# The first projections of a hybrid decoder step: token squares taken from the feature blocks of x, four like passes for v, and later row loads

## The chip, the cores and the metric

The kernel runs on one core of one Trainium2 chip. The metric is the time of one launch on the device, in microseconds (us), as the median of several runs. Beside the runs there is one profiled execution, whose trace is read here; it has its own time.

## The reference, cut to what matters

One decoder layer is computed for 256 prompt tokens and 64 sampled tokens (8 sequences of 8), 320 tokens together, with a model width of 2048. Everything is float32.

```python
def rms_norm(x, w):
    y = xf * lax.rsqrt(jnp.mean(xf * xf, axis=-1, keepdims=True) + EPS)
    return (y * w).astype(x.dtype)

def decoder_layer(x, ...):
    h = rms_norm(x, p["norm_mix_pre"])
    proj = h @ p["w_in"]                       # columns: u | v | z | x,B,C | dt
    gate_out, chunk_v = chunk_spatial_gate(a_u, a_v, ...)   # v = layer_norm(gelu(a_v))
    ssm_out, ... = ssd_mixer(z, xbc, dt_raw, ...)           # xbc: causal conv of width 4, silu
    mix = concat([gate_out, ssm_out]) @ p["w_out"]
    x = x + rms_norm(mix, p["norm_mix_post"])
    f, ... = conv_ffn(rms_norm(x, p["norm_ffn_pre"]), ...)
    x = x + rms_norm(f, p["norm_ffn_post"])
```

What the change touches is the beginning: the norm of x, the 2048 columns of `a_v` (2048 to 4095 of `w_in`), the layer norm of v, and the conv inputs B and C.

## The kernel before, in words

**Layout.** Activations are held transposed: features on the 128 partitions, the 320 tokens along the free axis. x comes in as `xT`, 16 blocks of 128 features by 320 tokens (160 KB each), and a second time by token as `x_tok` for the sum of squares. A product with float32 accuracy is made from three passes in a faster format: each operand is split into a high part (a rounded copy) and a low part (the difference), and `accumulate` (line 128) issues high by high (L130), high weights by low x (L131) and low weights by high x (L132), each 128x128 weights against 128x320. `slab` (line 112) loads up to 512 KB of weights by SyncE (SP, L117), makes the rounded copy on ScalarE (ACT, L119) and the difference on VectorE (DVE, L121). Raw, high and low weights have three buffers each, so a load waits until the difference of the third slab before it is made, and a rounded copy waits until TensorE (PE) has used the third one before it.

**A pass.** `project` (line 154) multiplies all 16 blocks of h with 512 (or 256) columns of a weight matrix: 192 matmuls for 512 columns, into four PSUM banks (tag `mm`, four buffers). After each column block the evacuation `evac` is written out; after each slab `tick` advances one background task in the list `bg`. The norm's factor of a token, `r1`, is not needed for the matmuls, since it is multiplied in when a bank is evacuated: `scaled` (line 336) multiplies by `r1` on DVE (L340) and applies the activation on ACT (L341).

**Order.** The program is written by one Python thread with background generators and priorities (`tc.high_priority`, `first`); a scheduler then fixes a list of instructions for each engine, and each engine works through its list in order. `tc.issue_after` makes an instruction wait for another.

**The beginning.** The first pass over v (columns 2048 to 2559) loads x block by block in `x_ready` (L538), splits it on ACT (L543) and DVE (L544), and between these loads the token rows of x (L559), six loads of 256 or 512 KB. `x_squares` squares them on ACT with a running sum (L564), and `rsqrt_of` makes `r1` in eleven small DVE operations; `spread` (L269) turns it with three PE transposes and `r1` is copied out of PSUM on ACT (L271). The first pass does not wait for it: its four banks stay full (`late`), and the next 256 columns go to four banks of the other PSUM pool (`spare=True`, `misc`). When `r1` is there, the task `with_r1` issues the parameter loads (`params`, L329 to L332) and the four late evacuations. Then come 256 more columns and two passes of 512, with `turned` (12 PE transposes by L576, three copies by L577) after each group of 512 columns.

**After that** come the conv inputs B and C (`conv_proj`: the evacuation writes a padded row `pad` with three buffers, L393 and L394, then ACT L398 and three DVE steps L400), beside them the layer norm of v in the background (`layer_norm`, bn_stats L617, L635, L636), with its rows loaded by GpSimd (POOL, L628), then dt, the first x heads, and the gate's passes. The gate's weights for the first group (`gate_mix`, L653 to L655) are loaded by POOL as well. Both the first rows and the first gate weights wait for one small POOL copy of `r1` (`behind_r1`, L334).

Of the kernel before, what the change touches and what calls it, by code (L numbers as in the profile page):

```python
# [9 lines left out]
F32 = mybir.dt.float32  # L10
# [7 lines left out]
P = 128  # L18
NP = 256
# [15 lines left out]
def hybrid_step(  # L35
# [118 lines left out]
    def project(w, c0, evac, width=512, spare=False, late=None, quiet=0, ready=None, small=0, after=None, ahead=1, rate=1, more=None, held=None):  # L154

        nb = width // P
        ps = [misc(f"ps_{c0}_{j}") if spare else mm.tile([P, 512], F32, tag="mm", name=f"ps_{c0}_{j}") for j in range(nb)]
# [20 lines left out]
        there = None  # L178
        for cut in cuts[:ahead] if ready else []:
            there = ready(*cut)  # L180
        for i, (k0, nk) in enumerate(cuts):
            with tc.issue_after(there or after) if there or after and i > 1 else nullcontext():
                if ready and i + ahead < len(cuts):
                    there = ready(*cuts[i + ahead])
# [140 lines left out]
    behind_r1 = []  # L325

    def params():
        with tc.issue_after(slab_load[-1]):
            sp.dma_start(prm, cols)  # L329
            sp.dma_start(sst, sconv)  # L330
            sp.dma_start(bias_bc, ssm_dt_bias[0:1, :].broadcast_to([P, NH]))
            sp.dma_start(a_bc, ssm_a_log[0:1, :].broadcast_to([P, NH]))  # L332
        there = tp.tile([P, 1], F32, tag="there", name="r1_there", bufs=1)
        behind_r1.append(pool.tensor_copy(there, r1[:, 0:1]).ins)  # L334
# [37 lines left out]
    with ExitStack() as mctx:  # L372
# [6 lines left out]
        def conv_proj(c0, k0, out, soon=0):  # L379
# [138 lines left out]
        with tc.tile_pool(name="gp", bufs=1) as gp:  # L518
# [14 lines left out]
            x_split = []  # L533

            def x_ready(k0, nk):
                with tc.high_priority(offset=100000):
                    cs = slice(KD + NT * k0 if k0 else 0, KD + NT * (k0 + nk))
                    sp.dma_start(flat[:, cs], xT[:, cs])  # L538
                    for _ in range({4: 1, 6: 1, 8: 1, 10: 1, 12: 2}.get(k0, 0)):
                        load_by_token()  # L540
                    for kt in range(k0, k0 + nk):
                        x = xf[:, kt, :]
                        x_split.append(act.activation(hT[0][:, kt, :], x, AF.Copy, scale=pre[:, kt:kt + 1]).ins)  # L543
                        dve.scalar_tensor_tensor(out=hT[1][:, kt, :], in0=x, scalar=pre[:, kt:kt + 1],  # L544
                                                 in1=hT[0][:, kt, :].bitcast(F32), op0=ALU.mult, op1=ALU.subtract)


            ssq = gp.tile([P, 3, 2], F32, name="ssq1")
            pool.memset(ssq, 1.0)
            xp = acc.rearrange("p k n -> p (k n)")[:, :2 * D].rearrange("p (c d) -> p c d", c=2)  # L550
            by_tok = [(xp[:, c, D // 2 * i:D // 2 * (i + 1)], slice(0, P), slice(P * c, P * c + P), c, i)
                      for c in range(2) for i in range(2)]
            by_tok += [(t.rearrange("p k n -> p (k n)")[64:, :D // 2], slice(64, P), slice(NP, NT), 2, i) for i, t in enumerate((bT, cT))]
            to_load = list(by_tok)

            def load_by_token():
                if to_load:
                    t, _, rows, _, i = to_load.pop(0)
                    sp.dma_start(t, x_tok[rows, D // 2 * i:D // 2 * (i + 1)])  # L559

            def x_squares():
                for n, (t, at, _, c, i) in enumerate(by_tok):
                    with tc.high_priority(offset=50000), tc.issue_after(x_split[min(15, 11 + n)]):
                        act.activation(t, t, AF.Square, accum_out=ssq[at, c, i:i + 1])  # L564
                with first():
                    ss1 = gp.tile([P, 3], F32, name="ss1")
                    dve.tensor_reduce(out=ss1, in_=ssq, axis=mybir.AxisListType.X, op=ALU.add)
                    return rsqrt_of(ss1, 1.0 / D, 3)
# [12 lines left out]

            late = []
            project(w_in, V0, lambda j, ps: scaled(ps, AF.Gelu, vfs[0][:, j, :]), ready=x_ready, small=4, ahead=0, late=late)
            with tc.high_priority(offset=100000):
                while to_load:
                    load_by_token()

            def with_r1():
                yield
                yield  # L590
# [7 lines left out]
            task = with_r1()  # L598
            next(task)
            bg.append(task)  # L600
# [47 lines left out]
            def gate_mix(g, uf, res):  # L648
# [3 lines left out]
                with tc.issue_after(behind_r1[0]):  # L652
# [652 lines left out]
```

## Time and profile before

| | |
|---|---|
| runs (median; lowest, highest) | 1795.4 us; 1794.08, 1796.96 (3 runs) |
| profiled execution, its own time | 1796.46 us |
| span of its instructions | 1794.8 us |
| granted TensorE clock, mean | 0.998 |
| PE, DVE, ACT, POOL busy | 99%, 66%, 44%, 15% |
| moved by DMA | 306.45 MB, 171 GB/s on average |

The profile gives, for each engine, the busy time and the number of instructions; PEld is the weight load of TensorE, which runs beside its matmuls. A view of windows gives the same for chosen stretches, in brackets the number of instructions that touch the stretch. A line of the timeline reads: start, duration, engine and line, operation, output and inputs, shapes, count, and in square brackets the idle time before it with what ended it. A matmul's own record is about 0.31 us long, but matmuls overlap, so PE's rate is read from the number of records in a stretch and not from its busy share.

### The profile page before, as it was taken

How to read it: one execution, taken by the hardware profiler on the slowest of the kernel's cores; microseconds unless marked ns; L12 is line 12 of the kernel's file. 1: busy time of each engine (PE TensorE's matmuls, PEld its weight loads, DVE VectorE, ACT ScalarE, POOL GpSimd, SP SyncE). 2: the span in 40 equal slices, each digit the busy share in tenths (PEclk: the TensorE clock that was granted, in tenths of full speed). 3: DMA queues.
4: the chain of work that ended last, by engine and by line, in shares of the span. 5: the costliest groups of instructions: out<-in, count | busy, mean ns of one | idle time of the engine just before them, and what ended most of it. 6: DMA issues, size and time to landing. Idle time of an engine off the chain costs nothing.

```text
span 1794.8 us, 31242 instructions
## 1 busy us (share of the span) xinstructions
PE 1777.0 (99%) x12235; PEld 1744.6 (97%) x12235; DVE 1186.1 (66%) x2051; ACT 796.4 (44%) x1105; POOL 268.0 (15%) x591
## 2 busy tenths in 40 slices
PE   8999999999999999999999999999999999999998
PEld 8999999999989898999999999999999999999997
DVE  5449565556867778677876575767666575656565
ACT  6444454334535354445645443443434343433334
POOL 1102110000220111003222212121101020101004
PEclk9999999999999999999999999999999999999999
DMA  8645544445764654454565656566554444444442
GB/s 274 185 142 178 174 139 154 153 152 163 242 195 157 192 159 153 138 170 150 161 198 199 206 177 192 191 193 213 173 190 152 150 155 153 151 148 153 154 152 98
DMA packets 230210, 306.45 MB, mean 171 GB/s; under 512 B 17488, under 2 KB 153008, under 8 KB 229872
## 3 DMA queue, kind: packets, MB, share of 16 engines
q1 hardware_dynamic: 218416, 284.51, 49.8%
q10 hardware_dynamic: 10160, 15.47, 2.3%
q0 software_dynamic: 1488, 4.49, 0.9%
q8 instruction: 96, 1.57, 0.4%
q14 instruction: 50, 0.41, 0.1%
HBM read 286.85 MB, written 17.58 MB: 170 GB/s over the span
## 4 chain that ended last, share of the span: by engine, by line
PE 89%; issue 6%; DMA 3%; DVE 1%; ACT 1%; SPq 0%; POOL 0%; DVEq 0%; POOLq 0%; ACTq 0%
PE ps L130 18%; PE ps L132 18%; PE ps L131 18%; PE pd L130 10%; PE pd L132 10%; PE pd L131 10%; PE y_ps L862 1%; DMA wraw<-in_w_in 1%; DMA vt<-in_xT 1%; PE yo_ps L815 1%; PE sg L669 0%; PE up_ps L1155 0%; PE tsum L261 0%; PE xt_ps L361 0%; DVE wlo L121 0%
## 5 line engine op out<-in xcount | busy, mean ns | idle before, releaser
L121 DVE TENSOR_TENSOR wlo<-wraw,whi 128x1024 fp32r<-128x1024 f32 x472 | 587.6, 1245 | 393.9 <-ACT whi L119 391.3
L119 ACT CAST whi<-wraw 128x1024 fp32r<-128x1024 f32 x472 | 494.1, 1047 | 719.7 <-PE ps L131 429.0
L130 PE MATMUL ps<-h_hi,whi 128*128 128x320 f32 x2528 | 785.2, 311 | 5.2 <-ACT whi L119 3.6
L131 PE MATMUL ps<-h_lo,whi 128*128 128x320 f32 x2528 | 780.5, 309 | 0.0
L132 PE MATMUL ps<-h_hi,wlo 128*128 128x320 f32 x2528 | 779.2, 309 | 0.4 <-DVE wlo L121 0.4
L130 PEld LDWEIGHTS ps<-h_hi,whi 128*128 128x128 f32 x2528 | 474.8, 188 | 11.7 <-issue 5.3
L131 PEld LDWEIGHTS ps<-h_lo,whi 128*128 128x128 f32 x2528 | 475.1, 188 | 1.5 <-issue 0.5
L132 PEld LDWEIGHTS ps<-h_hi,wlo 128*128 128x128 f32 x2528 | 474.5, 188 | 1.8 <-DVE wlo L121 1.3
L130 PE MATMUL pd<-fhi,whi 128*128 128x320 f32 x704 | 217.4, 309 | 0.0
L132 PE MATMUL pd<-fhi,wlo 128*128 128x320 f32 x704 | 217.3, 309 | 0.0
L131 PE MATMUL pd<-flo,whi 128*128 128x320 f32 x704 | 217.3, 309 | 0.0
L130 PE MATMUL pd<-ohi,whi 128*128 128x320 f32 x448 | 140.5, 314 | 0.0
L131 PE MATMUL pd<-olo,whi 128*128 128x320 f32 x448 | 138.9, 310 | 0.0
L132 PE MATMUL pd<-ohi,wlo 128*128 128x320 f32 x448 | 138.6, 309 | 0.0
L131 PEld LDWEIGHTS pd<-flo,whi 128*128 128x128 f32 x704 | 132.2, 188 | 0.7
L132 PEld LDWEIGHTS pd<-fhi,wlo 128*128 128x128 f32 x704 | 132.2, 188 | 0.0
L130 PEld LDWEIGHTS pd<-fhi,whi 128*128 128x128 f32 x704 | 132.2, 188 | 0.0
L213 DVE TENSOR_TENSOR acc_ffn<-acc_ffn,pd 128x320 f32<-128x320 f32 x160 | 77.1, 483 | 34.6 <-PE pd L132 33.6
L130 PEld LDWEIGHTS pd<-ohi,whi 128*128 128x128 f32 x448 | 84.1, 188 | 4.0 <-issue 2.5
L132 PEld LDWEIGHTS pd<-ohi,wlo 128*128 128x128 f32 x448 | 84.1, 188 | 0.6 <-issue 0.6
L131 PEld LDWEIGHTS pd<-olo,whi 128*128 128x128 f32 x448 | 84.2, 188 | 0.2 <-issue 0.2
L1052 POOL COPY ptf<-pad 128x2 f32<-128x2 f32 x88 | 21.0, 240 | 408.1 <-DVE pad L1040 407.6
(292 smaller groups left out, 1572.1 us busy)
## 6 DMA issues: line engine op xcount, KB each, us to landing
wraw<-in_ffn_w_up SPq DMA_DIRECT2D x176, 512.0 KB, 3.5
wraw<-in_w_in SPq DMA_DIRECT2D x144, 512.0 KB, 3.5
wraw<-in_ffn_w_down SPq DMA_DIRECT2D x88, 512.0 KB, 3.3
wraw<-in_w_out SPq DMA_DIRECT2D x64, 512.0 KB, 3.3
st<-in_state_ssm SPq DMA_DIRECT2D x64, 256.0 KB, 3.6
out_ssm_state_sample<-st ACTq DMA_DIRECT2D x32, 256.0 KB, 2.4
cs<-dacs_d SPq DMA_DIRECT2D x16, 320.0 KB, 3.6
xr<-in_xT SPq DMA_DIRECT2D x4, 640.0 KB, 4.6
```

What stands on the lines that cost most here:

```text
L119: act.copy(hi[:, :m], raw[:, :m])
L121: dve.tensor_tensor(out=lo[:, :m], in0=raw[:, :m], in1=hi[:, :m].bitcast(F32), op=ALU.subtract)
L130: pe.matmul(ps, whi, xhi, start=first, stop=False)
L131: pe.matmul(ps, whi, xlo, start=False, stop=False)
L132: return pe.matmul(ps, wlo, xhi, start=False, stop=last).ins
L213: dve.tensor_tensor(out=acc[:, nb, :], in0=acc[:, nb, :], in1=ps[:, :NT], op=ALU.add)
L815: pe.matmul(ps_yo[row:row + 32, :256], cms[:, 4 * h + i, :], st[h][:, 256 * r:256 * r + 256], start=i == 0, stop=i == 3, tile_position=(0, ...
L862: pe.matmul(ps[64 * i:64 * i + 64, cols], w(hl), x(hl, m, cpx), tile_position=(0, 64 * i), **flags)
L1052: pool.tensor_copy(ptf[:, k, :], pad[:, 256:258])
```

## The change

- x is loaded once, as `xT`, in more and earlier pieces; `x_tok` is no longer read by the kernel. The squares are made from the feature blocks: ACT squares two blocks at a time into `acc` (8 operations of 128x640), DVE adds them up (7 of 128x640 and one of 128x320), and `token_sums` adds over the partitions with three PE matmuls of one column each.
- The four groups of v are four like passes of 512 columns in the `mm` banks. The first one evacuates after `r1`, which is made within it: the new argument `before=tick` advances the task with `spread` and `params` ahead of its first evacuation.
- The transposes of group g come after the pass of group g+1, the last ones inside the pass of B, as a background task ahead of the layer norm.
- The layer norm's rows wait for the third group of v, the gate's first weights for the first block of B, each through a small POOL copy (`behind`).
- Odd blocks of B and C take up to three more padded buffers, cut from a buffer of `xs`.

```diff
@@ project
-                if kt == KD - 1 and late is None:
+                if kt == KD - 1 and late is None and not before:
+            if before and kt == KD - 1:
+                if js[0] == 0:
+                    before()
+                for j in js:
+                    evac(j, ps[j])
...
+        to_make = list(cuts) if ready else []
         for i, (k0, nk) in enumerate(cuts):
+            with tc.issue_after(after) if after and i > 1 else nullcontext():
+                while to_make and len(cuts) - len(to_make) <= max(i + ahead, (i + 1) * (i == len(cuts) - 2)):
+                    ready(*to_make.pop(0))
@@ conv
-                pad = op.tile([P, LP], F32, tag="pad", name="pad", bufs=3)
+                pad = spare_pads.pop(0) if spare_pads and j % 2 else op.tile([P, LP], F32, tag="pad", name="pad", bufs=3)
@@ x_ready
-                    sp.dma_start(flat[:, cs], xT[:, cs])
-                    for _ in range({4: 1, 6: 1, 8: 1, 10: 1, 12: 2}.get(k0, 0)):
-                        load_by_token()
+                    for at in {0: (0,), 1: (1,), 2: (2,), 3: (3,), 4: (4, 6), 6: (8, 10), 8: (12, 14)}.get(k0, ()):
+                        x_load(at, 1 if at < 4 else 2)
...
+                with tc.high_priority(offset=50000):
+                    for kt in range(k0 - k0 % 2, k0 + nk - 1, 2):
+                        act.activation(acc[:, kt:kt + 2, :], xf[:, kt:kt + 2, :], AF.Square)
+                        if kt:
+                            dve.tensor_tensor(out=acc[:, 0:2, :], in0=acc[:, 0:2, :], in1=acc[:, kt:kt + 2, :], op=ALU.add)
@@ with_r1
-                    r = x_squares()
+                    dve.tensor_tensor(out=acc[:, 0, :], in0=acc[:, 0, :], in1=acc[:, 1, :], op=ALU.add)
+                    r = rsqrt_of(token_sums(acc[:, 0, :]), 1.0 / D, 3)
                 yield
                 spread(r, r1)
                 params()
-                for ev, j, ps in late:
-                    ev(j, ps)
@@ the passes of v
-            project(w_in, V0 + 512, lambda j, ps: scaled(ps, AF.Gelu, vfs[1][:, j, :]), width=256, spare=True)
-            turned(0, vfs[0])
-            project(w_in, V0 + 768, lambda j, ps: scaled(ps, AF.Gelu, vfs[1][:, 2 + j, :]), width=256)
-            turned(1, vfs[1])
+            v_pass(0, vfs[0], ready=x_ready, small=4, ahead=0, before=tick)
+            v_pass(1, vfs[1])
+            turned(0, vfs[0])
             for g in range(2, 4):
                 vf = gp.tile([P, 4, NT], F32, tag="vf", name="vf", bufs=2)
-                project(w_in, V0 + 512 * g, lambda j, ps: scaled(ps, AF.Gelu, vf[:, j, :]))
-                turned(g, vf)
+                v_pass(g, vf)
+                turned(g - 1, vfs[-1])
+                vfs.append(vf)
+                if g == 2:
+                    behind(vf[:, 3, 0:1])
+            def last_turned():
+                yield
+                turned(3, vfs[-1])
+            bg.append(last_turned())
@@ layer_norm, gate_mix, the conv passes
-                        with tc.issue_after(behind_r1[0]):
+                        with tc.issue_after(after_v[0]):
...
-                with tc.issue_after(behind_r1[0]):
+                with tc.issue_after(after_v[-1]):
...
+            spare_pads = op.tile([P, 4, NT], F32, tag="xs", name="xs_pads", bufs=2).rearrange("p k n -> p (k n)")
+            spare_pads = [spare_pads[:, LP * i:LP * i + LP] for i in range(3)]
             conv_proj(B0, 16, lambda j: bT[:, j, :], 50000)
+            behind(bT[:, 0, 0:1])
```

More of the change, by code (lines that the diff above doesn't have):

```diff
@@ L152, in finish, with project @@
             tick()
-    def project(w, c0, evac, width=512, spare=False, late=None, quiet=0, ready=None, small=0, after=None, ahead=1, rate=1, more=None, held=None):
+    def project(w, c0, evac, width=512, late=None, before=None, quiet=0, ready=None, small=0, after=None, ahead=1, rate=1, more=None, held=None):
         nb = width // P
-        ps = [misc(f"ps_{c0}_{j}") if spare else mm.tile([P, 512], F32, tag="mm", name=f"ps_{c0}_{j}") for j in range(nb)]
+        ps = [mm.tile([P, 512], F32, tag="mm", name=f"ps_{c0}_{j}") for j in range(nb)]
         if more:
@@ L323, in hybrid_step @@
     sst = cp.tile([P, 24, NB, 3], F32, name="sst")
-    behind_r1 = []
     def params():
@@ L332, in params @@
             sp.dma_start(a_bc, ssm_a_log[0:1, :].broadcast_to([P, NH]))
-        there = tp.tile([P, 1], F32, tag="there", name="r1_there", bufs=1)
-        behind_r1.append(pool.tensor_copy(there, r1[:, 0:1]).ins)
     def scaled(ps, func, out):
@@ L549, in hybrid_step @@
[L549 to L568, printed above, removed]
+                with tc.high_priority(offset=50000):
[3 more added lines that the diff above has]
+                            dve.tensor_tensor(out=acc[:, 0:2, :], in0=acc[:, 0:2, :], in1=acc[:, kt:kt + 2, :], op=ALU.add)
@@ L580, in hybrid_step @@
             first_raw += [vf.rearrange("p k n -> p (k n)")[:, 512 * i:512 * i + 512] for vf in vfs for i in range(2)]
[L582 to L586, printed above, removed]
             def with_r1():
-                yield
-                yield
+                yield from repeat(None, 7)
                 with first():
-                    r = x_squares()
+                    dve.tensor_tensor(out=acc[:, 0, :], in0=acc[:, 0, :], in1=acc[:, 1, :], op=ALU.add)
+                    r = rsqrt_of(token_sums(acc[:, 0, :]), 1.0 / D, 3)
                 yield
@@ L595, in with_r1, with behind, v_pass @@
                 params()
[L596 to L601 removed]
+                yield
+            after_v = []
+            def behind(x):
+                there = tp.tile([P, 1], F32, tag="there", name="v_there", bufs=1)
+                after_v.append(pool.tensor_copy(there, x).ins)
+            r1_task = with_r1()
+            bg.append(r1_task)
+            def v_pass(g, vf, **more):
+                project(w_in, V0 + 512 * g, lambda j, ps: scaled(ps, AF.Gelu, vf[:, j, :]), **more)
+            v_pass(0, vfs[0], ready=x_ready, small=4, ahead=0, before=tick)
+            v_pass(1, vfs[1])
             turned(0, vfs[0])
[L603 to L604 removed]
             for g in range(2, 4):
                 vf = gp.tile([P, 4, NT], F32, tag="vf", name="vf", bufs=2)
[L607 to L608 removed]
+                v_pass(g, vf)
[4 more added lines that the diff above has]
+            def last_turned():
+                yield
+                turned(3, vfs[-1])
+            bg.append(last_turned())
             def layer_norm():
```

16 lines of the change are left out of this document (6 added, 10 removed).

## The prediction

> **What bounds the kernel now.** I read the page first, then PE's waits, then windows cut at the ends of the passes, then the timeline at each wait.
>
> ```profile
> span 1794.8 us, 31242 instructions
> PE 1777.0 (99%) x12235; PEld 1744.6 (97%) x12235; DVE 1186.1 (66%) x2051; ACT 796.4 (44%) x1105; POOL 268.0 (15%) x591
> PE 89%; issue 6%; DMA 3%; DVE 1%; ACT 1%; SPq 0%; POOL 0%; DVEq 0%; POOLq 0%; ACTq 0%
> ```
>
> PE is busy all the time and is 89% of the chain that ended last. The change takes no work from PE; it adds three small matmuls. So all it can win is time in which PE stood still, and the list of PE's waits says how much there is in the part that it touches:
>
> ```profile
> PE ps L130 <- ACT whi L119: 3.6, 3, 2.5
> PE vt_ps L576 <- ACT vf L341: 1.6, 1, 1.6
> PE ps L130 <- DVE pad L394: 1.3, 1, 1.3
> ```
>
> The windows give the same as a balance. They are cut at the ends of the four v groups, of B and of C (the columns: window, its length, each engine's busy time with its instructions, granted clock, DMA share, GB/s).
>
> ```profile
> 4.90:40.35 35.45, 31.53 (x192) 29.47 (x193) 21.89 (x40) 23.77 (x39) 3.32 (x7) 0.95 0.87 288
> 40.35:70.60 30.25, 30.17 (x209) 29.72 (x208) 12.69 (x18) 13.92 (x20) 5.66 (x11) 1.00 0.80 231
> 70.60:102.00 31.40, 29.77 (x206) 29.38 (x205) 14.30 (x16) 11.97 (x16) 0.00 (x0) 1.00 0.44 135
> 102.00:131.70 29.70, 29.70 (x206) 29.45 (x205) 12.87 (x14) 11.62 (x15) 0.00 (x0) 1.00 0.47 142
> 131.70:161.40 29.70, 29.70 (x206) 29.45 (x205) 26.89 (x52) 11.28 (x14) 3.09 (x8) 1.00 0.56 165
> 161.40:191.10 29.70, 28.41 (x194) 28.17 (x193) 24.45 (x44) 14.50 (x22) 9.48 (x20) 1.00 0.65 208
> 191.10:219.20 28.10, 28.10 (x194) 28.10 (x193) 15.65 (x21) 11.85 (x18) 5.41 (x13) 1.00 0.49 151
> ```
>
> The last window is a pass without any wait: 192 matmuls (two more touch its edges) in 28.10 us, 0.146 us each. The window 102.00:131.70 is such a pass with its 12 transposes: 29.70. Against these, the first pass lost 35.45 - 28.10 = 7.35; the second, which also holds three transposes of `spread`, about 0.3; the third 31.40 - 29.70 = 1.70; C 29.70 - 28.10 = 1.60. Together 10.95 us: the most that the change can win.
>
> **The first pass, before.** Its loss is late data:
>
> ```profile
> 14.84 0.33 SPq L538 DMA_DIRECT2D vt<-in_xT  x1
> 19.67 1.04 ACT L119 CAST whi<-wraw 128x1024 fp32r<-128x1024 f32 x1 [1.76 <-DMA wraw<-in_w_in]
> 27.01 0.56 ACT L543 ACTIVATE h_hi<-vt 128x320 fp32r<-128x320 f32 x1 [2.33 <-DMA vt<-in_xT]
> 31.09 0.41 PE L130 MATMUL ps<-h_hi,whi 128*128 128x320 f32 x1 [2.49 <-ACT whi L119]
> 31.20:35.00 3.80, 3.56 (x14) 3.15 (x15) 2.11 (x3) 3.77 (x7) 1.31 (x1) 0.55 0.49 146
> ```
>
> The last four blocks of x were issued at 14.84 and used from 27.01; behind them ACT also had token squares in front of the weights' copy, and PE stood 2.49 us. Then came 3.8 us at a granted clock of 0.55, with 14 matmuls where 26 fit (3.80 / 0.146): 1.7 us more. [...] The trace shows the clock at 1.00 in all other windows above and low just behind the one long gap, so I count it with the gap.
>
> **The first pass, after.** The queue is relieved of 2.5 MB. At the 288 GB/s of the window that is 2,560 KB / 288 = 9.1 us of transfer ahead of the last blocks; x and the pass's weights alone are 2.6 + 4.2 MB, 24 us at that rate, with x at the front (the last pieces and all ahead of them are 5.3 MB, 18 us), against a PE that wants the last four blocks at 4.97 + 144 x 0.146 = 26. So loads no longer set the pass. Next late is DVE, which gets seven adds of 128x640, a shape that the trace lacks:
>
> ```profile
> L121 DVE TENSOR_TENSOR wlo<-wraw,whi 128x1024 fp32r<-128x1024 f32 x56 | 68.4, 1222 | 69.1 <-ACT whi L119 69.1
> L121 DVE TENSOR_TENSOR wlo<-vf,whi 128x512 fp32r<-128x512 f32 x4 | 2.8, 692 | 1.2 <-ACT whi L119 1.2
> L544 DVE SCALAR_TENSOR_TENSOR h_lo<-vt,h_hi 128x320 fp32r<-128x320 f32 x16 | 8.7, 563 | 7.3 <-ACT h_hi L543 7.2
> L119 ACT CAST whi<-wraw 128x1024 fp32r<-128x1024 f32 x57 | 59.5, 1048 | 86.0 <-PE ps L131 66.8 <-DMA wraw<-in_w_in 12.3 <-issue 5.1
> L543 ACT ACTIVATE h_hi<-vt 128x320 fp32r<-128x320 f32 x16 | 8.5, 557 | 6.8 <-DMA vt<-in_xT 6.8
> L119 ACT CAST whi<-vf 128x512 fp32r<-128x512 f32 x4 | 2.5, 620 | 1.3 <-DMA vf<-in_w_in 1.0 <-DVE wlo L121 0.2
> 3.75 0.55 DVE L544 SCALAR_TENSOR_TENSOR h_lo<-vt,h_hi 128x320 fp32r<-128x320 f32 x1 [2.67 <-ACT h_hi L543]
> 4.97 0.41 PE L130 MATMUL ps<-h_hi,whi 128*128 128x320 f32 x1 [0.29 <-ACT whi L119]
> ```
>
> An add lies between 0.69 (512 wide) and 1.22 (1024 wide); by width I take 0.83. DVE's list in the pass is 16 x 0.56 + 4 x 0.69 + 6 x 1.22 + 7 x 0.83 + 0.45 for two masks = 25.3 us. It begins at 3.75, so it is through at 29.1 if it never starves, and PE wants the last slab's low part at 4.97 + 168 x 0.146 = 29.5. DVE just holds. With adds at 0.69 it is 1.4 us ahead, at 1.22 it is 2.3 us late. Neighbouring records overlap by some 0.08 us, which gives back up to 2.5. Within the list two slabs come late. Ahead of the first 1024-wide low part stand two h_lo, an add and the masks; ahead of the third stand four h_lo and two adds, 4 x 0.56 + 2 x 0.83 + 1.22 = 5.1 us (4.5 with the overlaps) in the 3.5 us that PE needs for a slab, less a lead of about 0.5. I put the two at 0.25 and 0.5: 0.75 in all. ACT has 16 x 0.56 + 4 x 0.62 + 6 x 1.05 + 8 squares between 0.62 and 1.05 (0.73) = 23.6 us from about 3.2, through at 27: not late.
>
> **The chain to r1** is now inside the pass, and PE waits twice in it by position. `tsum` stands 9 matmuls into the second-last slab (4.97 + 153 x 0.146 = 27.3), behind DVE's last add, which stands behind all of the list above (29.1 less the overlaps, plus 0.46): a wait of 0 to 2.1, and I take 0.5, near the low end, since the waits before it have already moved PE back. From `tsum` to `spread` lie 22 matmuls, 3.2 us. DVE has eleven small operations and one 1.22 among them; before, these took:
>
> ```profile
> 35.30 0.16 DVE L567 TENSOR_REDUCE ss<-ssq 128x3 f32<-128x6 f32 x1 [1.72 <-ACT cT L564]
> 40.54 0.16 DVE L233 SCALAR_TENSOR_TENSOR rs_r<-rs_t,rs_r 128x3 f32<-128x3 f32 x1
> 51.73 0.23 ACT L462 ACTIVATE a_bc<-a_bc 128x32 f32<-128x32 f32 x1 [3.17 <-DMA a_bc<-in_ssm_a_log]
> 53.09 0.42 ACT L271 COPY r<-spread 128x320 f32<-128x320 f32 x1
> ```
>
> 5.4 us with three operations of 1.22 among them, so 5.4 - 2 x 1.15 = about 3.2 with one: a wait of 0.3. After `spread` 19 matmuls remain, 2.8 us; in them go the copy of r1 (0.42) and the first evacuation (0.5). So the next pass finds its first bank free. With 0.1 for the three one-column matmuls, the pass keeps 0.75 + 0.5 + 0.3 + 0.1 = 1.65 of its 7.35 us and **wins 5.7**.
>
> **Transposes one pass later.** The 1.70 of the third window is this:
>
> ```profile
> 54.43 0.73 POOL L628 DMA_DIRECT2D lg<-in_gate_ln_g  x1
> 57.80 0.57 POOL L655 DMA_DIRECT2D bs<-in_gate_b_s  x1
> 69.41 1.05 ACT L119 CAST whi<-wraw 128x1024 fp32r<-128x1024 f32 x1 [4.63 <-DMA wraw<-in_w_in]
> 72.68 0.98 PE L576 MATMUL vt_ps<-ident,vf 128*128 128x128 f32 x7 [1.62 <-ACT vf L341]
> ```
>
> POOL's seven loads between 54.43 and 58.4 held up weights; the weights' copy at 69.41 held up ACT, behind it stood the gelu, and PE's transposes waited for that gelu. After the change they read a group finished a pass earlier, so the **1.7** goes, and the 0.3 beside it. As many transposes are issued as before.
>
> **Rows and gate weights later.** The four first row loads come behind the third v group (about 92), where PE and the weights have the slack of a plain pass; the rows are first read beside B (about 130). The three gate loads come behind the first block of B, about 155, together with two later row loads. POOL's two small copies wait in its queue for ACT; behind the first stand only those loads, behind the second the pad of C's last block and two row loads, and by then that block of B is long out. The parameter loads move ahead too, on SP, between weight slabs; the last of them, `a_bc`, stands behind a slab that waits for DVE, and ACT's copy of r1 stands behind its use. At the lists' pace it lands about when `spread` ends. I count all of this at nothing: the cover is two slabs, 7 us, of weights made ahead. Without it, see the second rival.
>
> **Three more pads.** C's loss is the evacuation behind DVE's conv steps, since it waited for a padded row:
>
> ```profile
> 165.56 0.39 PE L130 MATMUL ps<-h_hi,whi 128*128 128x320 f32 x1 [1.28 <-DVE pad L394]
> ```
>
> With six rows, B's four blocks leave PSUM without waiting for conv. DVE's work there is the same, and the layer norm's start moves two slabs later into windows where DVE already has 26.89 and 24.45 of 29.70. Bounds: a gain of 1.6, or the same wait again and as much more. I take **1.6**, since it is the row's own wait and the pads take away what it waited for.
>
> **Sum**: 5.7 + 1.7 + 0.3 + 1.6 = 9.3 us off the profiled execution's own 1796.46, or 1787.2. The median shown is 1.06 below that execution, so the forecast for the median is 1795.4 - 9.3 = **1786.1**.
>
> **Rivals.** *DVE becomes the bound of the first pass.* If adds cost near 1.22 and the chain's waits take their upper ends, the pass keeps 0.75 + 2.3 + 2.1 + 1 of its loss, some 6, and wins about 1.2; the rest stays: 4.8 won, 1790.6. For it: the list is 25.3 us in 25.8; against: the overlaps. Chance 0.12.
>
> *The moved loads collide beside C.* The trace's row at 69.41 is the price of such a group: ACT stood 4.63 and PE 1.62 us. At 155 DVE and ACT are fuller, and PE could pay between 1.6 and 4.6, and the pads' 1.6 with it: 3.1 to 6.1 won, 1789.3 to 1792.3. [...] Chance 0.11; in part of it the gain sinks below 0.2%.
>
> *r1 comes late (slower).* All four banks of `mm` now wait for r1, where the kernel before had four others to go on with. Every microsecond that the copy of r1 ends after about 36 (the pass's end: 4.97 + 28.1 + 1.65, plus slack) is a microsecond of PE. If its chain kept its old time, 53.09 + 0.42 + 0.5 = 54.0, PE would stand 18 us, with a slow-clock stretch of 1.7: 1786.1 + 19.7 = 1806. It decides from a copy at about 45 on. For it: `a_bc` cost ACT 3.17 us at that place before; against: that is a third of what it takes, and the old chain waited for positions in PE's list and for token rows. Chance 0.05.
>
> **How the numbers follow.** About 0.2%, 3.6 us, is what a measurement here tells from no change. The forecast (7.5 to 11 won: 1784.4 to 1788) has 0.72; with the two rivals in between, faster is 0.72 + 0.12 + 0.05 = 0.89, same 0.06, slower 0.05. The range runs from 1784, all 10.95 of the loss won, to 1790.6, the first rival.
>
> **What the profile after would show.** A first pass of about 30 us with no gap over 1 us and the clock at 1.00; DVE busy nearly all of it; r1's copy near 33 to 36; no wait of `vt_ps` for a gelu and none of `ps` for a pad near 165. I am wrong if PE waits for `tsum` or `spread` by microseconds, if the first matmul of the second pass waits for an evacuation, or if weights come late near 95 or 160.

## The result, and the profile after

The changed kernel takes 1789.82 us (median of 8 runs, 1789.24 to 1791.3), the kernel before beside it on the same chip 1794.98 (8 runs, 1794.08 to 1797.58): a ratio of 0.997 with a 95% interval of 0.9959 to 0.9981, so 5.2 us faster. The profiled execution of the changed kernel took 1790.97 us, its span is 1789.3. The forecast was 1786.1 with a range from 1784.0 to 1790.6: the kernel is faster, as said, but by little more than half of the 9.3 us.

The head of the page and its chain, kernel after:

```profile
span 1789.3 us, 31254 instructions
PE 1775.5 (99%) x12241; PEld 1744.7 (98%) x12241; DVE 1191.2 (67%) x2058; ACT 794.3 (44%) x1101; POOL 276.6 (15%) x591
PE 92%; DVE 4%; DMA 1%; issue 1%; ACT 1%; POOL 0%; SPq 0%; DVEq 0%; ACTq 0%; POOLq 0%
```

PE's share of the chain went from 89 to 92%. The windows are cut at the ends of the same passes as before (the four v groups, B, C; all engines). The row of B now holds 24 transposes, those of its own place and the last group's. The row by itself, PE alone, is the stage of dt and X0, the first heads:

```profile
4.72:36.20 31.48, 30.71 (x202) 29.56 (x202) 27.79 (x51) 24.01 (x38) 6.75 (x13) 1.00 0.84 285
36.20:64.30 28.10, 28.10 (x194) 28.10 (x193) 11.60 (x12) 10.79 (x14) 0.00 (x0) 1.00 0.47 148
64.30:93.80 29.50, 29.50 (x206) 29.49 (x205) 12.78 (x14) 11.52 (x15) 0.00 (x0) 1.00 0.46 143
93.80:123.20 29.40, 29.40 (x206) 29.39 (x205) 12.78 (x14) 11.52 (x15) 3.12 (x5) 1.00 0.57 179
123.20:154.05 30.85, 30.85 (x218) 30.84 (x218) 23.98 (x46) 12.55 (x17) 2.46 (x5) 1.00 0.50 154
154.05:182.95 28.90, 28.82 (x194) 28.17 (x193) 25.26 (x45) 13.93 (x21) 13.12 (x18) 1.00 0.61 190
```

```profile
190.20:219.00 28.80, 26.72 (x183) 1.00 0.51 162
```

The first pass went from 35.45 to 31.48 us, 4.0 won where 5.7 was forecast. The second is now a bare 28.10, the third has no stall, and C takes 28.90 instead of 29.70: its first half runs at the pace of a pass without waits, its second half loses about 0.6. Counted by the place of a matmul in PE's list, PE is 8.8 us ahead in the middle of C (the 1056th matmul that is 320 wide starts at 168.17, before at 176.93). Then it gives 3 us back, up to the transposes of dt. PE's waits in the first 240 us name the place of most of it:

```profile
PE ps L130 <- DVE dtf L430: 2.1, 1, 2.1
PE ps L130 <- ACT whi L119: 0.6, 1, 0.6
```

`dtf` is the evacuation of dt's projection, whose bank the last block of X0 needs. The timeline shows why it came late; first POOL's queue, then DVE, ACT and PE (`vt` is the layer norm's data, `lb` a row that it reads):

```profile
163.90 0.09 POOL L389 MEMSET pad<- 128x3 f32 x1 [3.39 <-DVE cv L399]
163.94 5.77 POOL L390 COPY pad<-sst 128x24 f32<-128x24 f32 x1
169.66 0.54 POOL L622 DMA_DIRECT2D lb<-in_gate_ln_b  x1
170.60 0.54 POOL L622 DMA_DIRECT2D lb<-in_gate_ln_b  x1 [0.40 <-DVE vt L630]
165.79 2.06 DVE L630 SCALAR_TENSOR_TENSOR vt<-vt,rs_r,lb 128x512 f32<-128x512 f32 x3
173.95 0.75 DVE L630 SCALAR_TENSOR_TENSOR vt<-vt,rs_r,lb 128x512 f32<-128x512 f32 x1 [3.64 <-DMA lb<-in_gate_ln_b]
179.01 1.05 ACT L119 CAST whi<-wraw 128x1024 fp32r<-128x1024 f32 x1 [6.03 <-DVE vt L630]
194.38 0.50 DVE L430 TENSOR_TENSOR dtf<-ps_dt,r 32x320 f32<-32x320 f32 x1
194.93 0.41 PE L130 MATMUL ps<-h_hi,whi 128*128 128x320 f32 x1 [2.08 <-DVE dtf L430]
```

The two late row loads (`lb`, 256 KB each) stand in POOL's queue behind the preparation of C's last pad, which first waits for DVE's conv and then is recorded with a copy of 5.77 us. They have a second condition: `lb` has two buffers, so each load must wait until DVE has read the old row for the last time. For the first one that was so at 167.18, the end of the second of the three steps at 165.79; the second one left at 170.60, right behind DVE's reading (the 0.40 of its row). So the copy held up only the first load, and by some 2.2 us (169.66 against 167.18 and the 0.3 us of a release, measured at the second load: DVE's reading ends at 170.30, the load leaves at 170.60). The load then took 4.3 us to land, for which DVE stood 3.64: some 2.2 us of that come from the copy, the rest from the late release of the buffer. The layer norm ends late; ACT's issue of the outputs of v waits for it, with a weight copy behind (6.03). C's evacuations and conv then queue up on DVE, and `dtf` comes 2.08 us too late for PE. The remaining 0.9 us or so of the give-back are small gaps, most of them in the second half of C. In the kernel before the same two loads left at 155.64 and 157.63.

### The profile page after: what moved, and what is told of

Same layout as the page of the kernel before. It is cut to its first block, busy times and chain, and to the rows that moved or that the text cites. A ratio compares the mean times of both kernels' runs of the same rounds, so it can differ in the third digit from the quotient of the medians.

```text
span 1789.3 us, 31254 instructions
## 1 busy us (share of the span) xinstructions
PE 1775.5 (99%) x12241; PEld 1744.7 (98%) x12241; DVE 1191.2 (67%) x2058; ACT 794.3 (44%) x1101; POOL 276.6 (15%) x591
## 4 chain that ended last, share of the span: by engine, by line
PE 92%; DVE 4%; DMA 1%; issue 1%; ACT 1%; POOL 0%; SPq 0%; DVEq 0%; ACTq 0%; POOLq 0%
PE ps L130 19%; PE ps L132 19%; PE ps L131 19%; PE pd L130 10%; PE pd L132 10%; PE pd L131 10%; DVE wlo L121 1%; PE y_ps L859 1%; PE yo_ps L812 1%; PE tsum L264 0%; PE sg L663 0%; PE up_ps L1152 0%; DMA wraw<-in_w_in 0%; DVE acc_mix L998 0%; PE xt_ps L360 0%
```

## The experiments

All of them are edits of the changed kernel, unless said otherwise. Theory one, formed from the rows above, is the **row wait**. The theory as I formed it puts the whole wait on the copy ahead of the loads. Its rivals: a **collision** of the gate loads and outputs with the weights (the prediction's second rival), the **outputs** standing in ACT's queue, and the shared **bank** alone.

Two things make the comparison. The times: medians against the kernel before on the same chip. And a ruler inside the trace: the start of dt's five transposes (`dt_ps`), which have the same matmuls ahead of them in every version but for the small ones of `tsum`. This is the row of the first profile of before, and that of after (behind `x5` the shortest, middle and longest time in ns, then the start of the first and of the last):

```profile
L439 PE MATMUL dt_ps<-ident,dtf x5: 221/222/247, 226.5 to 226.7; 32*128 32x32 f32 x5
```

```profile
L438 PE MATMUL dt_ps<-ident,dtf x5: 221/222/244, 220.7 to 220.9; 32*128 32x32 f32 x5
```

The ratios are against the kernel before on the same chip, with medians of 1795.22 (e1 to e4), 1795.33 (e5 to e8) and 1796.45 us (e9 to e12).

| kernel | median, us | ratio to before (95%) | span | start of `dt_ps` | span less that |
|---|---|---|---|---|---|
| before | 1794.98 | | 1794.8 | 226.5 | 1568.3 |
| before, second profile (e9) | 1795.42 | 0.9997 (0.9986 to 1.0007) | 1793.5 | 224.5 | 1569.0 |
| after | 1789.82 | 0.997 (0.9959 to 0.9981) | 1789.3 | 220.7 | 1568.6 |
| e1 rows together | 1788.3 | 0.9967 (0.9954 to 0.9979) | 1786.6 | 217.2 | 1569.4 |
| e2 outputs late | 1791.59 | 0.9983 (0.9974 to 0.9992) | 1789.8 | 219.9 | 1569.9 |
| e3 dt in another bank | 1788.88 | 0.9968 (0.9956 to 0.9979) | 1786.9 | 218.2 | 1568.7 |
| e4 loads early | 1790.42 | 0.9974 (0.9964 to 0.9984) | 1788.6 | 218.7 | 1569.9 |
| e5 transposes early | 1789.19 | 0.9969 (0.9956 to 0.9982) | 1787.0 | 218.3 | 1568.7 |
| e6 no added pads | 1790.36 | 0.997 (0.9959 to 0.9981) | 1787.7 | 218.3 | 1569.4 |
| e7 before, with the pads | 1794.19 | 0.9996 (0.9986 to 1.0005) | 1791.5 | 223.0 | 1568.5 |
| e8 adds on POOL | 1797.0 | 1.001 (1.0 to 1.0019) | 1797.2 | 227.5 | 1569.7 |
| e10 thin adds | 1789.34 | 0.9965 (0.9953 to 0.9977) | 1789.7 | 220.3 | 1569.4 |
| e11 rows together, squares later | 1789.06 | 0.9963 (0.995 to 0.9975) | 1789.4 | 218.1 | 1571.3 |
| e12 rows together, no added pads | 1788.51 | 0.9956 (0.9941 to 0.9972) | 1787.3 | 217.7 | 1569.6 |

The last column is work behind the edits, and it varies by 3 us between executions. So a span alone misleads here (e11), and medians of versions within 1 us of each other are not told apart. The ruler is one execution for each version. It can be split at the 1056th wide matmul, in the middle of C: from there to `dt_ps` lie 49.52 us in before, e1, e5, e7 and e11 (e9: 49.53), 52.49 in after, 52.22 in e2, 51.05 in e4, 51.60 in e8, 53.59 in e10, and 49.80 to 49.85 in e3, e6 and e12. The give-back is what this stage has above 49.52.

**e1: all row loads together.** The four late rows get memory of their own and are issued with the first four:

```diff
-                        rows.append(gp.tile([P, 512], F32, tag=name, name=name, bufs=2))
+                        n = 2 * (q - 2) + (name == "lb")
+                        rows.append(gp.tile([P, 512], F32, tag=name, name=name, bufs=2) if q < 2 else
+                                    acc.rearrange("p k n -> p (k n)")[:, 512 * n:512 * n + 512])
...
-                load(0)
-                load(1)
+                for q in range(4):
+                    load(q)
```

> The changed kernel with all eight row loads of the layer norm issued together behind the third v group; the four late ones go into a part of the mix accumulator that is idle then, so none stands behind the pad's copy in POOL's queue or waits for a buffer. Everything else keeps its order. Theory one (the row wait: two `lb` loads stand behind the preparation of C's last pad in POOL's queue, DVE stands 3.64 us for them, the layer norm ends 3 us late, dt's evacuation with it, and PE waits 2.1 us for that): the 3.64 goes, PE's wait for `dtf` goes, span 1786.3 to 1787.2 against 1789.3. Theory two (collision: gate loads and outputs of v hold up weights on the shared DMA engines, and the row wait costs nothing): span 1788.8 to 1789.4, `dtf` still waited for.

```profile
189.43 0.50 DVE L430 TENSOR_TENSOR dtf<-ps_dt,r 32x320 f32<-32x320 f32 x1
L438 PE MATMUL dt_ps<-ident,dtf x5: 221/222/243, 217.2 to 217.5; 32*128 32x32 f32 x5
L390 POOL COPY pad<-sst 128x24 f32<-128x24 f32 x12 | 13.2, 1104 | 1.0 <-DMA sst<-in_sconv 1.0
```

`dtf` comes 5 us earlier, PE waits for it no more, and dt's transposes start 3.5 us earlier than in after (0.4 of that stems from the first pass of this execution). POOL's pad copies are as long as in after, 13.2 us for twelve (after 13.4), but nothing that matters stands behind them. The stage from the middle of C is back at the 49.52 us of before. The row wait is the cause of the give-back; the gate loads are where they were, so the collision isn't. The edit takes away both of its parts at once, the place behind the copy and the wait for a buffer; e6 shows the second one nearly alone.

**e2: outputs of v after X0's last weight copy** (recorded as `hi_made` in the weight helper).

```diff
-                act.dma_start(o_v_p[0, 0].rearrange("t h d -> t (h d)"), vt[:, 1, :])
-                act.dma_start(o_v_s[0].rearrange("b t h d -> (b t) (h d)"), vt[:NS, 2, :])
...
             finish(normed)
+            with tc.issue_after(hi_made[-1]):
+                act.dma_start(o_v_p[0, 0].rearrange("t h d -> t (h d)"), vt[:, 1, :])
+                act.dma_start(o_v_s[0].rearrange("b t h d -> (b t) (h d)"), vt[:NS, 2, :])
```

> The changed kernel with the two outputs of v issued after the last weight copy of the first X pass instead of at the layer norm's end. ACT no longer stands 6.0 us for the layer norm with weight copies behind it, and 1.5 MB no longer leave beside the weights of dt and X0. Theory one: the row wait of 3.64 us stays on DVE, so at most 0.5 to 1 us is won: 1788.3 to 1789.3. A third theory (outputs: ACT's stand and the transfers delay the weights at 186 and 190, and that delays dt's evacuation): PE's wait for `dtf` goes, 1786.5 to 1787.3.

```profile
173.17 0.75 DVE L631 SCALAR_TENSOR_TENSOR vt<-vt,rs_r,lb 128x512 f32<-128x512 f32 x1 [3.51 <-DMA lb<-in_gate_ln_b]
194.14 0.41 PE L131 MATMUL ps<-h_hi,whi 128*128 128x320 f32 x1 [1.83 <-DVE dtf L431]
```

ACT's 6 us are gone and no weight waits for its load there, yet DVE stands as long for the rows and PE as good as long for `dtf`: ACT's stand and the outputs were followers. The median is not better than after's.

**e3: dt's projection in another bank.**

```diff
-            ps_dt = mm.tile([P, 512], F32, tag="mm", name="ps_dt")
+            ps_dt = misc("ps_dt")
```

> The changed kernel with the bank of dt's projection taken from the four miscellaneous PSUM banks, so that X0's last block needs no evacuation of dt. The order of instructions is the same. If PE's loss there is only the bank: the 2.1 us go, and with the small gaps before it the span is 1786.4 to 1787.3. If the weights of X0 are late as well (collision): PE meets the next wait within a slab and 1 us or less is won, 1788.3 to 1789.3.

```profile
173.86 0.75 DVE L630 SCALAR_TENSOR_TENSOR vt<-vt,rs_r,lb 128x512 f32<-128x512 f32 x1 [3.33 <-DMA lb<-in_gate_ln_b]
193.13 0.50 DVE L430 TENSOR_TENSOR dtf<-ps_dt,r 32x320 f32<-32x320 f32 x1
```

DVE is as late as in after, and PE does not notice: `dt_ps` at 218.2. The lateness became PE's only through the bank, and no other wait stood right behind it.

**e4: row and gate loads behind r1, as before the change.**

```diff
                 spread(r, r1)
                 params()
+                behind(r1[:, 0:1])
...
-                if g == 2:
-                    behind(vf[:, 3, 0:1])
...
-            behind(bT[:, 0, 0:1])
```

> The changed kernel with row and gate loads released by the first r1 copy again, as before the change. Only POOL's order differs. Collision theory: without the gate loads at 159 the give-back shrinks to 1 us or less: 1786.5 to 1787.5. Row wait theory: the two late `lb` loads still stand behind the pad's copy, the 3.64 us of DVE and the 2.1 us of PE stay, and the early loads cost 0 to 1.7 us of PE near 70: 1789.3 to 1791.

```profile
173.13 0.75 DVE L629 SCALAR_TENSOR_TENSOR vt<-vt,rs_r,lb 128x512 f32<-128x512 f32 x1 [3.30 <-DMA lb<-in_gate_ln_b]
193.02 0.42 PE L130 MATMUL ps<-h_hi,whi 128*128 128x320 f32 x1 [1.00 <-DVE dtf L430]
```

The row wait stays, 3.30, and PE's wait falls to 1.00. The span, 1788.6, lies between what the two theories gave. The 1.1 us less for `dtf` is not separated from the spread of the transfers: e3, with the gate loads late, has `dtf` at 193.13, also 1.3 earlier than after. Near 70 PE meets no wait, but that is no test of the later transposes: the first load now leaves at 34.21, 20 us earlier than in the kernel before (54.43). The weights' copy that it holds up is another one, and no transposes stand behind that:

```profile
47.75 1.05 ACT L119 CAST whi<-wraw 128x1024 fp32r<-128x1024 f32 x1 [3.70 <-DMA wraw<-in_w_in]
```

**e5: transposes behind their own pass**, loads as late as in the change.

```diff
             turned(0, vfs[0])
+            turned(1, vfs[1])
             for g in range(2, 4):
...
-                turned(g - 1, vfs[-1])
+                turned(g, vf)
...
-            def last_turned():
-                yield
-                turned(3, vfs[-1])
-            bg.append(last_turned())
```

> The changed kernel with each v group's transposes right behind its own pass (groups 1 to 3 one pass earlier), the row and gate loads as late as in the change. The layer norm can start two slabs earlier, and POOL's queue has all row loads ahead of C's pads. Row wait theory: DVE's 3.64 us for `lb` and PE's wait for `dtf` go, 1786.4 to 1787.4. On the 1.7 us of the third pass: if the late loads alone remove it, PE meets no wait for a gelu near 70 (0.3 at most); if the later transposes were needed for it, a wait of 1 to 1.7 us is back and the span is 1788 to 1789.

```profile
152.48 0.75 DVE L627 SCALAR_TENSOR_TENSOR vt<-vt,rs_r,lb 128x512 f32<-128x512 f32 x1 [0.45 <-DMA lb<-in_gate_ln_b]
64.06 3.15 PE L560 MATMUL vt_ps<-ident,vf 128*128 128x128 f32 x24
```

The layer norm starts earlier, its rows are used 21 us earlier with 0.45 of wait, and PE waits neither for `dtf` nor for a gelu. ACT stands for no late weight near 70, where it stood 4.63, 4.28 and 2.78 us in before, e9 and e7. So the later loads alone are enough to take away the wait of the third pass; whether the later transposes alone would be, no run here shows. It still loses 1.1 us to e1, in gaps of 0.15 to 0.25 us at each group and in the transposes (24 of them in 3.15 us, where after has 12 in 1.47).

**e6: without the three added pads.**

```diff
-            spare_pads = [spare_pads[:, LP * i:LP * i + LP] for i in range(3)]
+            spare_pads = []
```

> The changed kernel without the three added padded buffers. Prediction's term: C waits again for a pad, 1.3 to 1.6 us near 165; with the row wait as it is the span is 1790.3 to 1791. Rival: what the pads won is taken back at dt's evacuation anyway, since the same DVE work is only in another order: 1789.0 to 1789.6, with a smaller wait for `dtf`.

```profile
PE ps L130 <- DVE pad L393: 0.3, 1, 0.3
166.06 0.54 POOL L622 DMA_DIRECT2D lb<-in_gate_ln_b  x1 [0.22 <-issue]
170.11 1.42 DVE L630 SCALAR_TENSOR_TENSOR vt<-vt,rs_r,lb 128x512 f32<-128x512 f32 x2 [1.22 <-DMA lb<-in_gate_ln_b]
```

The wait for a pad is 0.3 us, not 1.3, and PE does not wait for `dtf` at all. POOL's list falls otherwise: the copy ahead of the rows takes 0.55 us here, the first load leaves as soon as its buffer is free, and DVE still stands 1.22 us. This is the part of the row wait that the two buffers make by themselves. Time and ratio are those of after; the span, 1787.7, is below the ranges of both theories, and the ruler is 2.4 us earlier than in after. So the figure of the prediction was wrong, and of the rival the idea holds, not the number: in the changed kernel the added pads won nothing.

**e7: the kernel before with the pads alone** (the same expression and its two lines put into it).

> The kernel before with the three padded buffers alone. Prediction's term: the wait of 1.28 us for a pad goes and some 0.3 beside it, and nothing comes back, since the layer norm is early there: 1793.1 to 1793.6 against 1794.8. Rival: a wait for `dtf` takes its place: 1794.5 to 1795.

```profile
PE ps L130 <- ACT whi L119: 3.8, 3, 2.9
PE early L70 <- DVE ones L66: 1.1, 1, 1.1
PE ps L132 <- DVE wlo L121: 0.6, 2, 0.4
```

This is all that PE waits for in the first 240 us: the wait for a pad is gone, as I expected, and nothing took its place. By time the two are not told apart (interval 0.9986 to 1.0005). The span, 1791.5, is below the range of 1793.1 to 1793.6, since there is also no wait of `vt_ps`, although nothing was changed there.

**e8: the seven adds on POOL.**

```diff
-                            dve.tensor_tensor(out=acc[:, 0:2, :], in0=acc[:, 0:2, :], in1=acc[:, kt:kt + 2, :], op=ALU.add)
+                            pool.tensor_tensor(out=acc[:, 0:2, :], in0=acc[:, 0:2, :], in1=acc[:, kt:kt + 2, :], op=ALU.add)
```

> The changed kernel with the seven adds of 128x640 in the first pass on POOL instead of DVE. If DVE's list is what keeps the first pass at 31.5 us: the gaps of PE near 14 and 21.5 (0.23 and 0.30 us above pace) go, with the small ones beside them, the pass takes 30.3 to 31.0, and the span is 1788.3 to 1788.8 as long as POOL's adds end by 26. If the pass's loss is ACT's order and the loads at its start: 31.3 to 31.6 still. If POOL's adds are slow: PE waits for `tsum`, 0.5 to 3 us.

```profile
18.28 11.35 POOL L552 TENSOR_TENSOR acc_mix<-acc_mix 128x640 f32<-128x640 f32 x6
17.28 4.90 DVE L546 SCALAR_TENSOR_TENSOR h_lo<-vt,h_hi 128x320 fp32r<-128x320 f32 x4
22.11 2.56 DVE L121 TENSOR_TENSOR wlo<-wraw,whi 128x1024 fp32r<-128x1024 f32 x1
24.73 0.41 PE L132 MATMUL ps<-h_hi,wlo 128*128 128x320 f32 x1 [2.35 <-DVE wlo L121]
```

A miss: the first pass takes 39.4 us, and the kernel is no faster than the one before (interval of the ratio 1.0 to 1.0019). None of my three cases had this: beside POOL's adds, four `h_lo` take 4.90 us instead of 4 x 0.55, a low part 2.56 instead of 1.22, and PE stands 2.35 us for it. Since the adds slowed DVE's other steps, this is no test of whether DVE's list sets the pass; e10 is.

**e9: the kernel before, a second profile.**

> The kernel before, unchanged: a second profiled execution. If the waits that the prediction took from the first one belong to the kernel, they stand here too: 2.5 us for a weight copy near 31 with 1.7 us of slow clock behind it, 1.6 us of `vt_ps` for a gelu near 72, 1.3 us for a pad near 165; total of the first 220 us within 0.5 us of 10.95. If one of them was that execution's own luck with its transfers, it is missing here and the span is shorter by as much: without the wait of `vt_ps` 1793.1.

```profile
PE ps L130 <- ACT whi L119: 2.4, 2, 2.0
PE ps L130 <- DVE pad L394: 1.3, 1, 1.3
PE vt_ps L576 <- ACT vf L341: 1.3, 1, 1.3
```

All three waits stand here again, each but the pad's smaller, with a stretch of half clock behind the first (0.66 on average from 30 to 35), and dt's transposes start 2.0 us earlier than in the first profile. So the total is not within 0.5 us of 10.95. With e7, `vt_ps` has waited 1.6, 1.3 and 0 us in three executions of what is the same code up to there.

**e10: thin adds**, `[:, 0:2, :8]` for `[:, 0:2, :]` and so on. The kernel leaves out most of the sum of squares.

> The changed kernel with the seven adds of squares cut to 8 of 320 columns each (so the norm's sums are not computed over all blocks: only the time counts). If DVE's list is what keeps the first pass above 28.1: 7 x 0.7 = 5 us of it go, the waits near 14 and 21 go, `tsum` and `spread` no longer wait, and the pass takes 29.6 to 30.4 instead of 31.4; span 1 us shorter, 1787.5 to 1788.5, with the row wait as it is. If it is ACT's order and the loads at the start: 31.0 to 31.5.

PE's only wait above 0.1 us in the first pass is one of 0.2 for a weight copy near 7. The pass, from its first matmul to the first of the next pass, takes 30.25 us. It takes 31.48 in after and 30.82 to 31.40 in e1 to e6 and e12, which have the same first pass. So DVE's adds cost 0.6 to 1.2 us of it, as the first theory has it. Beside dt this execution lost it again, 2.34 us for `dtf` and then a stretch at half clock, and its span is above the range:

```profile
193.10 0.64 PE L130 MATMUL ps<-h_hi,whi 128*128 128x320 f32 x1 [2.34 <-DVE dtf L430]
193.10:194.50 1.40, 1.40 (x5) 0.50 0.56 217
194.50:198.50 4.00, 4.00 (x24) 0.77 0.42 131
```

**e11: rows together, and the first two squares one place later on ACT** (with the edit of e1; `hi_made[-1]` is the last weights' copy).

```diff
-                    for kt in range(k0 - k0 % 2, k0 + nk - 1, 2):
-                        act.activation(acc[:, kt:kt + 2, :], xf[:, kt:kt + 2, :], AF.Square)
+                    for kt in {1: (), 2: (0,), 3: (), 4: (2, 4)}.get(k0, range(k0 - k0 % 2, k0 + nk - 1, 2)):
+                        with tc.issue_after(hi_made[-1]) if kt < 4 else nullcontext():
+                            act.activation(acc[:, kt:kt + 2, :], xf[:, kt:kt + 2, :], AF.Square)
```

> The changed kernel with all eight row loads issued together, and in the first pass the first two squares on ACT one place later, behind the weight copy that PE waits for near 7. Row wait theory: as in the run with the row loads alone, no wait for `dtf`. If ACT's square is what makes the early weight late: the gap near 7 (0.4 to 0.7 us) goes and the span is 1786.0 to 1786.4; if that weight's own load is late: 1786.6. Median 1787.6 to 1788.3.

A miss in time. There is no wait for `dtf`, as in e1. The weight near 7 is late all the same (a wait of 0.8 us for its copy), and with the squares moved `spread` waits 0.6 for r1's root. 0.9 us are lost against e1 by dt's transposes, and 1.9 more in the rest, much of them here:

```profile
645.42 0.80 PE L265 MATMUL tsum<-ones,ssq 128*128 128x1 f32 x6 [1.15 <-DVE ssq L283]
645.50:647.00 1.50, 1.50 (x10) 0.79 0.63 150
647.00:650.00 3.00, 3.00 (x14) 0.54 0.88 270
```

**e12: rows together, without the added pads** (the edits of e1 and e6).

> The changed kernel with all eight row loads issued together and without the three added padded buffers: the pads' term without the row wait. Prediction's term: C waits 1.3 to 1.6 us for a pad, span 1787.9 to 1788.3. Rival: with the layer norm two slabs later DVE reaches the pads sooner by itself, and the pads are worth 0.5 us or less: 1786.5 to 1787.1.

```profile
L438 PE MATMUL dt_ps<-ident,dtf x5: 221/222/245, 217.7 to 218.0; 32*128 32x32 f32 x5
PE ps L130 <- ACT whi L119: 0.3, 1, 0.3
```

No wait for a pad at all. It is 0.5 us behind e1 on the ruler, about half of it from the first two passes (its first transposes start at 64.25, those of e1 at 64.00). So with the layer norm two slabs later, the added pads are worth some 0.3 us at most, by one execution each. The rival had the mechanism; the span, 1787.3, is 0.2 above its range.

No version is shown to beat the changed kernel by time: their intervals overlap. On the ruler e1 is the earliest, 3.5 us ahead of after.

## Why the prediction was right or wrong

**Faster, and for the first reason given.** The loads of x no longer set the first pass, the clock is at 1.00 through it, and no gap in it is over 0.6 us by the waits. r1 was spread at 33.90 and the next pass began without a wait for an evacuation: the third rival, r1 late, did not come.

**The first pass: mis-sized, 4.0 instead of 5.7.** The adds took 0.82 us each (taken: 0.83):

```profile
L552 DVE TENSOR_TENSOR acc_mix<-acc_mix 128x640 f32<-128x640 f32 x7 | 5.7, 820 | 0.1
```

So DVE's list was sized right, and "two slabs come late" was right too: gaps of 0.23 and 0.30 us near 14 and 21 (taken: 0.25 and 0.5). `tsum` and `spread` came without the long waits that the first rival needs. What the sum lacked was the start (the first matmuls 0.43 and 0.27 us apart instead of 0.146, and a weight copy 0.56 us late near 7) and PE's own small steps for `tsum` and `spread` (`tsum` is recorded as six matmuls, not three). e10 shows that DVE's adds account for 0.6 to 1.2 of the 3.4 us that the pass has above 28.10, e11 that the order of ACT's squares is not the cause of the early weight. What holds that weight up, its own load or the x block ahead of it, stays open.

**The third pass and C: right in sum, wrong in the accounts.** The wait of `vt_ps` went, and so did C's for a pad. But the first goes with the late loads alone (e5), and the second has two edits that remove it alone, the pads (e7) or the later layer norm (e12). I gave the pads 1.6 us; behind the other edits they were worth some 0.3 at most, and with the rows as the change loads them nothing (e6). From the second pass to the middle of C, 0.9 us more came than forecast, partly since a pass with a group's transposes is 1.3 to 1.4 us longer than a bare one now (29.40 and 29.50 less 28.10), where it was 1.6. C's second half, already part of the give-back, lost 0.6 again.

**"I count all of this at nothing": the step that failed.** The prediction moved the row loads and named what stands ahead of them in POOL's queue: "behind the second the pad of C's last block and two row loads, and by then that block of B is long out". It looked at the release of the small copies, and not at how long the pad's own copy takes there (5.77 us), nor at the two buffers of `lb`: a late row can only be loaded when DVE has read the old one, and the layer norm that was moved back does so beside C, with nothing to do while the row lands. The cover that was named, two slabs of weights made ahead, covers late weights; the rows are used by DVE, which had no such cover. The price: 3.64 us on DVE, some 2.2 of it by the copy and the rest by the buffers, and 2.1 to 3 on PE. None of the signs that the prediction named for being wrong would have shown this. The second rival had the place (the stage beside C), the two loads and a price of 1.6 to 4.6 us, but the wrong cause: they did not hold up weights, they were held up themselves. In e1, where the same bytes are loaded and only the four late rows leave earlier, PE no longer waits for `dtf`.

**The base: 1 us.** The 10.95 us to be won were read in an execution that had lost 2 us more than another of the same kernel (226.5 against 224.5 at dt's transposes). The sum was made against that execution's 1796.46, but then taken off the median, 1795.4. Made against its own time, as the sum says, it gives 1787.2. On the ruler the forecast without any give-back is 226.5 - 9.3 = 217.2, and e1, the changed kernel without the row wait, is at 217.2. That is nearer than the terms deserve, since the first pass and the later ones miss in opposite directions.

**The clock.** I tied the 1.7 us of slow clock to the gap of 2.49 us. After the change the stretch is gone with the gap: the clock is 1.00 from 4.72 to 36.20. The length of a wait alone does not tell whether half clock follows: it stood behind waits of 2.0 (e9), 2.34 (e10) and 1.15 us (e11), none behind 2.08 (after). With before, e7 and e9, it stood behind the long wait of the first pass in all three executions of that code (2.49, 2.9 and 2.0 us), so counting it with the gap was right here.

## What to carry to other kernels

When a step is moved past others in a queue, ask of each instruction ahead of it what *that* one waits for and how long it takes in its new company, ask when the buffer that the step writes comes free, and follow the moved data to the engine that reads it: its slack is the cover, not that of the engine that sets the time. Where two edits remove the same wait, credit it once, and expect the second to bring nothing. A sum read from one execution belongs to that execution; a second profile of the unchanged kernel tells which of its waits are luck, and a mark in the trace ahead of untouched work compares versions better than whole spans do.

## What the runs showed of the hardware

In e8, with adds of 128x640 on POOL, DVE's steps beside them are longer: four `h_lo` took 4.90 us together and four more 5.85, where one is 0.55 in after, and a low part took 2.56, where it is 1.22. Up to 40 us an `h_lo` of e8 has 0.98 on average, a low part of 1024 columns 1.41 and one of 512 columns 0.93; in after they have 0.55, 1.22 and 0.69. The seven adds took 1.79 us each on POOL, and 0.82 on DVE in after. In after, a POOL copy of 24 columns is recorded with 5.77 us in a stretch in which DVE ran without a pause; three such copies into the added pads, at the start, have 0.2 each. What stretched it to 5.77 us was not tried by itself.

Half clock came in stretches of about 3.4 us here. In before it is 0.50 from 31.61 to 35.02. In e9 the clock is 0.66 from 30 to 35; in e10 it is 0.97 from 190.50 to 193.10, 0.50 up to 194.50 and 0.77 up to 198.50; in e11 it is 0.79 from 645.50 to 647 and 0.54 up to 650. At 0.50 each of these adds up to 3.4 us. The length of PE's wait does not tell whether such a stretch follows: it did behind 2.34 us (e10) and 1.15 (e11), and not behind 2.08 (after, 1.00 from 193.15 to 200), nor behind the waits of 1.1 in e10 and 1.2 in e9 in the stage of e11's 1.15 (1.00 from 646 to 660). In e4, e6 and e12 the clock is 0.91 from 820 to 840, where PE is idle for 0.25 us at most; in after it is 1.00 there, with 0.43 idle. What decides it no run here shows. In before such a stretch is worth 1.7 us (14 matmuls where 26 fit), in e11 1.6 (18 from 646 to 650, where before has 29, at 0.146 us each): about half of the 3.0 us by which the rest behind the edits is longer in e11 than in before.
